# Two output projections: plain float32 products in place of hi and lo parts

## The chip, the cores and the metric

The kernel runs on one core of a Trainium2 chip. The metric is the device time of one execution in microseconds (us); the median of the runs is compared.

## What is computed

Two transformer layers over 512 latent tokens and 256 context tokens, 1024 wide, all in float32. Layer 0 mixes tokens by grouped-query attention (16 heads of 64), layer 1 by latent attention (16 heads, values of 64). What matters here is the product behind each attention and the normalization after it:

```python
y_lat = block_attention(q_lat, k_all, v_all) @ w_o
y_ctx = block_attention(q_ctx, k_ctx, v_ctx) @ w_o if need_ctx else None
...
x = layer_norm(alpha * x + g_a * y_lat, ln_g[i, 0], ln_b[i, 0])
x = layer_norm(alpha * x + g_m * sq_relu_mlp(x * (1.0 + sc_m) + sh_m, mlp_w1[i], mlp_w2[i]), ...)
```

`w_o` is 1024 x 1024 in each layer. Layer 0 needs latent and context rows (768 tokens), layer 1 latent rows alone (512).

## The kernel before

Tokens are handled in tiles of 128: six in layer 0 (`range(NT)`), four in layer 1 (`range(NCT, NT)`). Most products keep float32 accuracy by splitting each operand into a hi part, a cast to float32r by ScalarE (`split_hi`, line 62), and a lo part, the float32 value less that cast, by VectorE (`split_lo`, line 65). Three products replace one: hi by hi, hi by lo, lo by hi (`mm3`, lines 88 to 91). Two kinds of work on TensorE use float32 as it is: the transposes (line 707 and others), and the attention's values (line 731), which multiply 64 columns for each of two heads into the two halves of one PSUM tile.

**Weights.** A weight goes by SP's DMA queue into one of three buffers named `raw` (line 69); its hi and lo parts go into rings of six `wh` and six `wl` tiles (lines 79 and 80). A slot is taken again when its last reader is done.

**The attention** (`Attn.run`, line 752) is a loop of rounds: scores of 128 queries for two heads, softmax, transposes of the probabilities, values. The order on TensorE is the program's; the other engines are ordered by the scheduler. At given steps of the loop (`at`) other work is put in. `early_weights` (lines 656 to 671) uses this: six of the eight 512 KB pieces of `w_o` are loaded (line 660) and some steps later split (lines 665 and 666, kept in program order). Result tiles `o`, one for each of eight head pairs, are 128 partitions by token tile by 128.

**The output projection** (`out_proj`, lines 881 to 936) has the eight pieces of the sum in `wts`; the last two are loaded and split into a pool of their own (line 904). For every token tile, the eight result pieces are split into `oh` and `ol` (lines 896 to 902), then for each k six products of 128 columns by 512 are summed in two PSUM tiles (lines 911 to 919):

```python
for k in range(KD):
    wh, wl = wts[k]
    for hf in range(2):
        ...
        nc.tensor.matmul(acc[hf], oh[k], wh[:, cs], start=(k == 0), stop=False)
        nc.tensor.matmul(acc[hf], oh[k], wl[:, cs], start=False, stop=False)
    for hf in range(2):
        ...
        nc.tensor.matmul(acc[hf], ol[k], wh[:, cs], start=False, stop=(k == KD - 1))
```

Behind them come the gate (line 924), the residual (line 925), the normalization (lines 304 to 314), the store of the row for later (line 929), and, for every two tiles, transposes and modulation into the MLP's operand (`to_act`, lines 331 to 362), which run in the time of the next tile. The MLP's first products (lines 975 to 979) follow on TensorE; its weights take the next slots of the same `wh` and `wl` rings.

Of the kernel before, what the change touches and what calls it, by code (L numbers as in the profile page):

```python
# [11 lines left out]
F32 = mybir.dt.float32  # L12
F32R = mybir.dt.float32r
# [6 lines left out]
P = 128  # L20
# [7 lines left out]
KD = D // P  # L28
# [11 lines left out]
def backbone(ctx, tc, a, out):  # L40
# [3 lines left out]
    nc = tc.nc  # L44

    def pool(stack, name, bufs=1, side="left", space=None):
        kw = {"space": space} if space is not None else {"side": side}
        return stack.enter_context(tc.tile_pool(name=name, bufs=bufs, reuse_waits="tile", **kw))

    const = pool(ctx, "const")  # L50
    wpool = pool(ctx, "wpool")
# [6 lines left out]
    def one():  # L58
        return ps.tile([P, 512], F32, name="one", tag="one", bufs=4)

    def split_hi(dst, src):
        return nc.scalar.copy(out=dst, in_=src)  # L62

    def split_lo(dst, src, hi):
        return nc.vector.tensor_tensor(out=dst, in0=src, in1=hi.bitcast(F32), op=ALU.subtract)  # L65

    def raw_tile(src, n):
        raw = wpool.tile([P, 1024], F32, name="raw", tag="raw", bufs=3)
        nc.sync.dma_start(raw[:, 0:n], src)
        return raw  # L70

    def weight(src, n=1024, wp=None, tiles=None, gate=None):
        raw = raw_tile(src, n)
        if gate is not None:
            nc.gpsimd.tensor_tensor(out=raw, in0=raw, in1=gate, op=ALU.mult)
        if tiles is not None:
            wh, wl = tiles
        elif wp is None:
            wh = wpool.tile([P, 1024], F32R, name="wh", tag="wh", bufs=6)
            wl = wpool.tile([P, 1024], F32R, name="wl", tag="wl", bufs=6)  # L80
        else:
            wh = wp.tile([P, 1024], F32R, name="wxh", tag="wxh", bufs=2)
            wl = wp.tile([P, 1024], F32R, name="wxl", tag="wxl", bufs=2)
        split_hi(wh[:, 0:n], raw[:, 0:n])
        split_lo(wl[:, 0:n], raw[:, 0:n], wh[:, 0:n])
        return wh, wl
# [278 lines left out]
    def stream(t):  # L365
        return 1 if t < NCT else 0
# [260 lines left out]
    for ch in range(1, 3):  # L627
        wts = [weight(a["w_qkv"][ch * 4 + i]) for i in range(4)]
        started.close()
        for t in range(NT):  # L630
            if (ch, t) in in_pairs:
                if t % 2 == 0:
                    pair = big()
                acc = pair[:, t % 2, :]
            else:
                acc = one()
# [10 lines left out]
            if kraw:  # L647
                kt, raw = kraw.popitem()
# [4 lines left out]
                assert not late  # L653
                st_k.close()

    def early_weights(src, ws, n, i0, i1, step, at):


        def load(k):
            ws.append(raw_tile(src[k], 1024))  # L660

        def split(k):
            raw = ws[k]
            wh, wl = (wpool.tile([P, 1024], F32R, name=nm, tag=nm, bufs=6) for nm in ("wh", "wl"))
            tc.keep_in_program_order(split_hi(wh, raw))
            tc.keep_in_program_order(split_lo(wl, raw, wh))
            ws[k] = wh, wl

        for k in range(n):
            at.setdefault(i0 + step * k, []).append(lambda k=k: load(k))  # L670
            at.setdefault(i1 + step * k, []).append(lambda k=k: split(k))

    class Attn:

# [182 lines left out]
    for k in range(KD):  # L857
        t = wpool.tile([P, D], F32, name="ada", tag="wh" if k < 6 else "wl", bufs=6)
# [6 lines left out]
    w_o0, at = [], {}  # L865

    for i, f in enumerate(ada_pe(0, 4, ada_ts, ada_bias4)):
        at.setdefault(0 + i, []).append(f)

    early_weights(a["w_o0"], w_o0, 6, 40, 46, 5, at)  # L870
    att.run(
        (0, QS0), prep0, scores0, lambda kt, h: V[:, kt, (h // 4) * 64 : (h // 4) * 64 + 64], o_of0, 8,
        ctx_scores0, fill, at,
# [7 lines left out]
    def out_proj(layer, wsrc, early, tiles, col0, o_of, x_src, x_dst, wxp, aH, aL, A, B, lnst, zst, x_ln):  # L881

        zp = pool(zst, "zp", side="right")
        ln = LN(lnst, layer, 0, 2, 1)
        if x_ln is not None:
            ln.gain(x_ln)
        wts = early + [weight(wsrc[k]) for k in range(len(early), 6)]
        temp = lambda: zp.tile([P, 512], F32, name="v", tag="v", bufs=2)  # L890
        ln.gate_tile(stream(tiles[0]))
        zs, late = [], []
        for t in tiles:
            s = stream(t)
            oh, ol = [], []
            for k in range(KD):
                h = ln.lp.tile([P, P], F32R, name="oh", tag="oh", bufs=12)
                l = ln.lp.tile([P, P], F32R, name="ol", tag="ol", bufs=12)
                split_hi(h, o_of(k)[:, t, :])
                split_lo(l, o_of(k)[:, t, :], h)  # L900
                oh.append(h)
                ol.append(l)
            if len(wts) < KD:
                wts += [weight(wsrc[k], wp=wxp) for k in range(6, KD)]
            z = zp.tile([P, D], F32, name="z", tag="z", bufs=3)
            x = ln.x_tile(x_src(t))
            if x_ln is not None:
                ln.affine(x, x)
            g = ln.gate_tile(s)
            acc = [one(), one()]  # L910
            for k in range(KD):
                wh, wl = wts[k]
                for hf in range(2):
                    cs = slice(hf * 512, hf * 512 + 512)
                    nc.tensor.matmul(acc[hf], oh[k], wh[:, cs], start=(k == 0), stop=False)  # L915
                    nc.tensor.matmul(acc[hf], oh[k], wl[:, cs], start=False, stop=False)  # L916
                for hf in range(2):
                    cs = slice(hf * 512, hf * 512 + 512)
                    nc.tensor.matmul(acc[hf], ol[k], wh[:, cs], start=False, stop=(k == KD - 1))  # L919
            while late:  # L920
                late.pop(0)()
            for hf in range(2):
                cs = slice(hf * 512, hf * 512 + 512)
                nc.vector.tensor_tensor(out=z[:, cs], in0=acc[hf], in1=g[:, cs], op=ALU.mult)
            nc.vector.scalar_tensor_tensor(
                out=z, in0=x, scalar=ALPHA, in1=z, op0=ALU.mult, op1=ALU.add
            )
            ln.norm(z)
            nc.sync.dma_start(x_dst[t * P : (t + 1) * P, :], z)
            zs.append(z)  # L930
            if len(zs) == 2:
                col = (t - 1) * P - col0
                late += ln.to_act(zs, col, s, A, B, aH, aL, temp, pin=t == tiles[-1])
                zs = []
        ln.close_x()
        return late
# [158 lines left out]
    A01, B01 = mod_ab(0, 1, 0)  # L1095
    st_ln, st_z = ExitStack(), ExitStack()
    late = out_proj(0, a["w_o0"], w_o0, range(NT), 0, o_of0, x_rows, xres[0], wx, aH, aL, A01, B01, st_ln, st_z, None)
    st_ln.close()
    st_wx.close()
# [105 lines left out]
    for t in range(NCT, NT):  # L1205
        acc = one()
        cols = slice(t * P, (t + 1) * P)
        for k in range(KD):
            wh, wl = wcq[k // 2]
# [58 lines left out]
    for t in range(NT):  # L1268
        cols = slice(t * P, (t + 1) * P)
        for hf in range(2):  # L1270
            acc = one()
            cs = slice(hf * 512, hf * 512 + 512)
# [39 lines left out]
    for c in range(4):  # L1312
        for j in range(2):
            q1[2 * c + j] = qo.tile([P, NLT, 192], F32, name=f"q1_{2 * c + j}", tag="qo1", bufs=9)
        for t in range(NLT):
# [5 lines left out]
            acc = one()  # L1321
            cols = slice(t * P, (t + 1) * P)
            for k in range(3):
                u = c * 3 + k
                wh, wl = wuq[u // 2]
# [36 lines left out]
    def o_of1(pr):  # L1362
# [2 lines left out]
        return o1[pr]  # L1365

    w_o1, at = [], {}
    early_weights(a["w_o1"], w_o1, 6, 20, 25, 6, at)
    att.run(first1, prep1, scores1, lambda kt, h: V1[:, kt, h * 64 : h * 64 + 64], o_of1, 8, None, None, at)
    st_att.close()  # L1370
    st_aq.close()
# [6 lines left out]
    A11, B11 = mod_ab(1, 1, 2)  # L1378
    st_ln, st_z = ExitStack(), ExitStack()
    late = out_proj(  # L1380
        1, a["w_o1"], w_o1, range(NCT, NT), CTX, o_of1, lambda t: xres[1][t * P : (t + 1) * P, :], xres[2], wx,
        aH, aL, A11, B11, st_ln, st_z, 1,
# [120 lines left out]
```

## Time and profile before

| | |
|---|---|
| three runs | 1687.68, 1688.68, 1694.34 us (median 1688.68) |
| the profiled execution | 1685.56 us, of which the span is 1683.8 |
| mean granted TensorE clock | 0.991 |

The span runs from the first to the last instruction; the 1.76 us between it and the execution's own time lie around it. Engines are PE (TensorE's products), PEld (its weight loads), DVE (VectorE), ACT (ScalarE), POOL (GpSimd) and SP (the queue that issues the DMAs). Starts of products are measured, their ends are modelled, so the spacing of starts tells more than a duration. A view that gives "idle before" names in brackets how long the engine stood and what ended that.

### The profile page before, as it was taken

How to read it: one execution, taken by the hardware profiler on the slowest of the kernel's cores; microseconds unless marked ns; L12 is line 12 of the kernel's file. 1: busy time of each engine (PE TensorE's matmuls, PEld its weight loads, DVE VectorE, ACT ScalarE, POOL GpSimd, SP SyncE). 2: the span in 40 equal slices, each digit the busy share in tenths (PEclk: the TensorE clock that was granted, in tenths of full speed). 3: DMA queues.
4: the chain of work that ended last, by engine and by line, in shares of the span. 5: the costliest groups of instructions: out<-in, count | busy, mean ns of one | idle time of the engine just before them, and what ended most of it. 6: DMA issues, size and time to landing. Idle time of an engine off the chain costs nothing.

```text
span 1683.8 us, 23748 instructions
## 1 busy us (share of the span) xinstructions
PE 1620.3 (96%) x9266; PEld 1364.3 (81%) x9266; DVE 1113.3 (66%) x1700; ACT 721.6 (43%) x1317; POOL 449.4 (27%) x317
## 2 busy tenths in 40 slices
PE   8997998999999999999999899999999899999996
PEld 6875776788888888998899798888878788888884
DVE  4778788766656775556448766766658655555577
ACT  3324677645532453342121356666653522222221
POOL 0247889000422444233104531000004200000034
PEclk9999999999999999999999999999999999999998
DMA  8312112223443464443122222001022432332322
GB/s 321 140 64 94 58 52 100 83 94 130 159 138 100 138 198 166 138 140 135 64 75 72 73 94 91 1 1 38 26 99 103 162 101 100 100 100 88 100 75 76
DMA packets 51969, 172.05 MB, mean 102 GB/s; under 512 B 6776, under 2 KB 6928, under 8 KB 51856
## 3 DMA queue, kind: packets, MB, share of 16 engines
q1 hardware_dynamic: 51824, 170.51, 30.1%
q8 instruction: 73, 1.20, 0.3%
q14 instruction: 40, 0.33, 0.1%
q10 hardware_dynamic: 32, 0.02, 0.0%
HBM read 161.03 MB, written 9.47 MB: 101 GB/s over the span
## 4 chain that ended last, share of the span: by engine, by line
PE 78%; DVE 11%; ACT 4%; DMA 3%; POOL 2%; issue 1%; DVEq 0%; SPq 0%; ACTq 0%; POOLq 0%
PE one L89 9%; PE one L91 9%; PE one L90 9%; PE big L975 7%; PE big L979 7%; PE big L978 7%; PE one L731 6%; PE one L707 4%; PE one L915 2%; DVE wl L65 2%; PE one L919 2%; PE one L916 2%; POOL xr L208 2%; DMA raw<-in_mlp_w_dram 2%; DVE yacc L1059 1%
## 5 line engine op out<-in xcount | busy, mean ns | idle before, releaser
L62 ACT CAST wh<-raw 128x1024 fp32r<-128x1024 f32 (+3 forms) x172 | 171.9, 1016 | 399.7 <-PE one L91 213.9
L65 DVE TENSOR_TENSOR wl<-raw,wh 128x1024 fp32r<-128x1024 f32 (+3 forms) x172 | 218.2, 1283 | 169.1 <-ACT wh L62 167.8
L975 PE MATMUL big<-actH,wh 128*128 128x384 f32 (+2 forms) x800 | 280.5, 351 | 4.8 <-ACT wh L62 4.8
L979 PE MATMUL big<-actH,wl 128*128 128x384 f32 (+2 forms) x800 | 279.6, 350 | 0.6 <-DVE wl L65 0.6
L978 PE MATMUL big<-actL,wh 128*128 128x384 f32 (+2 forms) x800 | 279.6, 350 | 0.0
L89 PE MATMUL one<-wh,hh 128*128 128x512 f32 x640 | 256.1, 401 | 11.3 <-ACT hh L62 6.8
L90 PE MATMUL one<-wl,hh 128*128 128x512 f32 x640 | 255.7, 400 | 1.3 <-DVE wl L65 1.3
L91 PE MATMUL one<-wh,hl 128*128 128x512 f32 x640 | 254.5, 399 | 2.1 <-DVE hl L65 2.1
L1057 DVE TENSOR_TENSOR yacc<-yacc,one 128x512 f32<-128x512 f32 x260 | 174.4, 683 | 112.2 <-PE one L91 111.9
L208 POOL TENSOR_TENSOR xr<-xr,raw 128x1024 f32<-128x1024 f32 x49 | 129.3, 2639 | 243.4 <-ACT raw L206 227.7
L975 PEld LDWEIGHTS big<-actH,wh 128*128 128x128 f32 x800 | 150.1, 188 | 18.5 <-ACT wh L62 6.0
L979 PEld LDWEIGHTS big<-actH,wl 128*128 128x128 f32 x800 | 150.1, 188 | 13.6 <-DVE wl L65 1.0
L978 PEld LDWEIGHTS big<-actL,wh 128*128 128x128 f32 x800 | 150.2, 188 | 12.2 <-issue 0.4
L89 PEld LDWEIGHTS one<-wh,hh 128*128 128x128 f32 x640 | 122.1, 191 | 42.7 <-ACT hh L62 7.9
L91 PEld LDWEIGHTS one<-wh,hl 128*128 128x128 f32 x640 | 121.3, 190 | 31.6 <-DVE hl L65 2.8
L90 PEld LDWEIGHTS one<-wl,hh 128*128 128x128 f32 x640 | 122.0, 191 | 27.6 <-DVE wl L65 1.7
L328 POOL TENSOR_TENSOR xr<-xr,ln_g 128x1024 f32<-128x1024 f32 x14 | 36.7, 2622 | 391.8 <-PE one L919 242.0
L691 ACT ACTIVATE prob<-big,nm 128x768 f32<-128x768 f32 x128 | 115.9, 909 | 56.2 <-DVE nm L690 55.9
L690 DVE TENSOR_REDUCE nm<-big 128x1 f32<-128x768 f32 x128 | 119.5, 953 | 14.7 <-PE big L1358 8.6
L707 PE MATMUL one<-ident,prob 128*128 128x128 f32 x832 | 103.2, 273 | 1.7 <-ACT pT L710 1.7
L707 PEld LDWEIGHTS one<-ident,prob 128*128 128x128 f32 x832 | 94.9, 141 | 5.2 <-ACT pT L710 2.2
L731 PE MATMUL one<-pT,V 128*64 128x256 f32 x768 | 96.8, 387 | 2.1 <-DVE pT L712 2.1
(245 smaller groups left out, 2823.4 us busy)
## 6 DMA issues: line engine op xcount, KB each, us to landing
raw<-in_mlp_w_dram SPq DMA_DIRECT2D x128, 512.0 KB
raw<-in_w_ada_dram SPq DMA_DIRECT2D x56, 512.0 KB
sraw<-in_w_ada_dram SPq DMA_DIRECT2D x16, 512.0 KB
araw<-in_w_ada_dram SPq DMA_DIRECT2D x32, 256.0 KB
raw<-in_w_o_dram SPq DMA_DIRECT2D x16, 512.0 KB
xr<-xres SPq DMA_DIRECT2D x14, 512.0 KB
raw<-in_w_qkv_dram SPq DMA_DIRECT2D x12, 512.0 KB
xres<-z SPq DMA_DIRECT2D x10, 512.0 KB
```

Of the source, the lines that this page charges most:

```text
L62: return nc.scalar.copy(out=dst, in_=src)
L65: return nc.vector.tensor_tensor(out=dst, in0=src, in1=hi.bitcast(F32), op=ALU.subtract)
L89: nc.tensor.matmul(o, lh, rh, start=start, stop=False)
L90: nc.tensor.matmul(o, lh, rl, start=False, stop=False)
L91: nc.tensor.matmul(o, ll, rh, start=False, stop=stop)
L208: nc.gpsimd.tensor_tensor(out=accs[s], in0=accs[s], in1=dst, op=ALU.add)
L707: nc.tensor.transpose(tp[:, j * P : (j + 1) * P], pts[j % 2][:, k * P : (k + 1) * P], ident)
L731: nc.tensor.matmul(acc[64 * hh : 64 * hh + 64, 0:256], v(kts[n], hh), PT[:, :, n, hh, :], start=(n == 0), stop=(n == len(kts) - 1),)
L975: mm = nc.tensor.matmul(o, wh[:, ks], aH[:, k, s:e], start=(k == 0), stop=False)
L978: nc.tensor.matmul(o, wh[:, ks], aL[:, k, s:e], start=False, stop=False)
L979: nc.tensor.matmul(o, wl[:, ks], aH[:, k, s:e], start=False, stop=(k == KD - 1))
L1057: nc.vector.tensor_tensor(out=yacc[i][:, cs], in0=yacc[i][:, cs], in1=accs[hf], op=ALU.add)
```

## The change

Operands of both output projections stay float32. The pieces of `w_o` are loaded by the new `o_weight` straight into slots of the rings, the first six under the tag `wh`, the last two under `wl`; `raw` is not used for them. The splits of the weights and of the attention's results go, and with them the second set of steps of `early_weights`. In layer 0 one product takes 128 columns; in layer 1 two products of 64 columns write the two halves of the PSUM tile's partitions.

```diff
-    def early_weights(src, ws, n, i0, i1, step, at):
-        def load(k):
-            ws.append(raw_tile(src[k], 1024))
-        def split(k):
-            raw = ws[k]
-            wh, wl = (wpool.tile([P, 1024], F32R, name=nm, tag=nm, bufs=6) for nm in ("wh", "wl"))
-            tc.keep_in_program_order(split_hi(wh, raw))
-            tc.keep_in_program_order(split_lo(wl, raw, wh))
-            ws[k] = wh, wl
+    def o_weight(src, k):
+        w = wpool.tile([P, 1024], F32, name="wo", tag="wh" if k < 6 else "wl", bufs=6)
+        nc.sync.dma_start(w, src)
+        return w
+
+    def early_weights(src, ws, n, i0, step, at):
         for k in range(n):
-            at.setdefault(i0 + step * k, []).append(lambda k=k: load(k))
-            at.setdefault(i1 + step * k, []).append(lambda k=k: split(k))
+            at.setdefault(i0 + step * k, []).append(lambda k=k: ws.append(o_weight(src[k], k)))
...
-    early_weights(a["w_o0"], w_o0, 6, 40, 46, 5, at)
+    early_weights(a["w_o0"], w_o0, 6, 40, 5, at)
...
-        wts = early + [weight(wsrc[k]) for k in range(len(early), 6)]
+        wts = early + [o_weight(wsrc[k], k) for k in range(len(early), KD)]
...
+        m = 64 if layer else P
         for t in tiles:
             s = stream(t)
-            oh, ol = [], []
-            for k in range(KD):
-                h = ln.lp.tile([P, P], F32R, name="oh", tag="oh", bufs=12)
-                l = ln.lp.tile([P, P], F32R, name="ol", tag="ol", bufs=12)
-                split_hi(h, o_of(k)[:, t, :])
-                split_lo(l, o_of(k)[:, t, :], h)
-                oh.append(h)
-                ol.append(l)
-            if len(wts) < KD:
-                wts += [weight(wsrc[k], wp=wxp) for k in range(6, KD)]
...
             for k in range(KD):
-                wh, wl = wts[k]
                 for hf in range(2):
                     cs = slice(hf * 512, hf * 512 + 512)
-                    nc.tensor.matmul(acc[hf], oh[k], wh[:, cs], start=(k == 0), stop=False)
-                    nc.tensor.matmul(acc[hf], oh[k], wl[:, cs], start=False, stop=False)
-                for hf in range(2):
-                    cs = slice(hf * 512, hf * 512 + 512)
-                    nc.tensor.matmul(acc[hf], ol[k], wh[:, cs], start=False, stop=(k == KD - 1))
+                    for i in range(0, P, m):
+                        nc.tensor.matmul(
+                            acc[hf][i : i + m], o_of(k)[:, t, i : i + m], wts[k][:, cs],
+                            start=(k == 0), stop=(k == KD - 1),
+                        )
...
-    early_weights(a["w_o1"], w_o1, 6, 20, 25, 6, at)
+    early_weights(a["w_o1"], w_o1, 6, 20, 6, at)
```

## Rows read from the trace of the kernel before

**Rows 1.** The page, parts 1 (busy, share, instructions) and 4 (chain by engine).

```profile
PE 1620.3 (96%) x9266; PEld 1364.3 (81%) x9266; DVE 1113.3 (66%) x1700; ACT 721.6 (43%) x1317; POOL 449.4 (27%) x317
...
PE 78%; DVE 11%; ACT 4%; DMA 3%; POOL 2%; issue 1%; DVEq 0%; SPq 0%; ACTq 0%; POOLq 0%
```

**Rows 2.** Windows of both output projections; columns as its first line says.

```profile
core 0: us, PE busy (x) PEld busy (x) DVE busy (x) ACT busy (x) POOL busy (x), PEclk, DMA share, GB/s
1252.70:1298.70 46.00, 46.00 (x206) 37.13 (x205) 37.04 (x65) 20.19 (x46) 21.01 (x11) 1.00 0.38 133
329.00:399.00 70.00, 70.00 (x316) 56.56 (x315) 41.25 (x103) 30.17 (x71) 2.77 (x5) 1.00 0.32 112
```

**Rows 3.** TensorE's timeline (start, us, what): first products of both projections, and behind.

```profile
328.46 0.51 PE L915 MATMUL one<-wh,oh 128*128 128x512 f32 x1 [0.72 <-ACT oh L62]
...
399.91 0.34 PE L975 MATMUL big<-actH,wh 128*128 128x384 f32 x1
...
1251.98 0.51 PE L915 MATMUL one<-wh,oh 128*128 128x512 f32 x1 [0.71 <-ACT oh L62]
...
1298.93 0.28 PE L975 MATMUL big<-actH,wh 128*128 128x256 f32 x1
```

**Rows 4.** The chain in order of time (start, us): transposes inside the projections.

```profile
386.86 1.81 PE one L341 x16
...
1285.94 1.81 PE one L341 x16
```

**Rows 5.** TensorE's timeline, one group of values, cut at three places.

```profile
318.23 0.44 PE L731 MATMUL one<-pT,V 128*64 128x256 f32 x2
...
318.23 0.87 PE L731 MATMUL one<-pT,V 128*64 128x256 f32 x6
...
318.23 1.51 PE L731 MATMUL one<-pT,V 128*64 128x256 f32 x12
```

**Rows 6.** Line 707, transposes: all records (ns min/median/max), and one group.

```profile
L707 PEld LDWEIGHTS one<-ident,prob x832: 137/141/146, 133.5 to 1246.0; 128*128 128x128 f32 x167
L707 PE MATMUL one<-ident,prob x832: 270/272/331, 133.6 to 1246.1; 128*128 128x128 f32 x167
...
312.74 1.47 PE L707 MATMUL one<-ident,prob 128*128 128x128 f32 x12
```

**Rows 7.** The chain in order of time, layer 0's attention: weight subtractions.

```profile
256.81 1.13 DVE wl L65
...
279.81 2.08 DVE wl L65
```

**Rows 8.** TensorE's timeline at those two places: where it stood idle.

```profile
257.70 0.55 PE L610 MATMUL one<-ident,q 128*128 128x128 f32 x3 [0.75 <-ACT pT L710]
...
282.54 1.52 PE L731 MATMUL one<-pT,V 128*64 128x256 f32 x12 [1.30 <-DVE pT L712]
286.07 0.33 PE L152 MATMUL one<-ident,modrow 128*128 128x128 f32 x1 [1.41 <-DVE modrow L132]
```

**Rows 9.** Window of layer 1's attention around one early split; columns as in rows 2.

```profile
1140.00:1165.00 25.00, 24.64 (x173) 20.44 (x172) 16.84 (x24) 16.66 (x36) 0.00 (x0) 1.00 0.07 22
```

**Rows 10.** TensorE's timeline: the last product with a key weight.

```profile
1210.56 0.34 PE L91 MATMUL one<-CKH,wl 128*128 128x384 f32 x1
```

**Rows 11.** VectorE's timeline before layer 0's MLP; the chain inside layer 1's MLP.

```profile
397.43 1.23 DVE L65 TENSOR_TENSOR wl<-raw,wh 128x1024 fp32r<-128x1024 f32 x1 [0.86 <-ACT wh L62]
...
1318.85 4.55 DVE wl L65 x2
```

**Rows 12.** Timeline of products and weight loads at 328.80.

```profile
328.80 0.39 PE L916 MATMUL one<-wl,oh 128*128 128x512 f32 x1
328.80 0.19 PEld L915 LDWEIGHTS one<-wh,oh 128*128 128x128 f32 x1
```

**Rows 13.** Windows with the granted clock; columns as in rows 2.

```profile
130.00:135.00 5.00, 2.52 (x24) 1.60 (x16) 4.94 (x13) 3.46 (x10) 2.76 (x3) 1.00 0.75 306
135.00:140.00 5.00, 3.44 (x27) 1.95 (x27) 4.91 (x12) 2.31 (x9) 2.53 (x3) 0.75 0.00 0
...
1241.90:1251.90 10.00, 9.37 (x77) 6.11 (x75) 3.16 (x7) 5.24 (x13) 0.00 (x0) 1.00 0.00 0
```

## The prediction

> **What bounds the kernel now.** The page first: TensorE is busy 96% of the span and holds 78% of the chain that ended last, while VectorE holds 11% [rows 1]. So what counts is TensorE's own time, and elsewhere only what TensorE waits for. Then the stretches of the two output projections by engine: TensorE is busy 70.00 of 70 us and 46.00 of 46 us, at the full granted clock, with VectorE at 59% and 81% and ScalarE below half [rows 2]. Inside them nothing that ScalarE, VectorE or a transfer does is waited for, so an instruction taken from those engines there buys nothing by itself. Last, the TensorE timeline gives the price of the work: layer 0 runs from 328.46 to 399.91, layer 1 from 1251.98 to 1298.93 [rows 3], with two and one groups of 16 transposes of 1.81 us in between [rows 4] (layer 0's other group is equal). That leaves 71.45 - 3.62 = 67.83 us for 6 tiles x 8 k x 6 = 288 products, 0.2355 us each, and 46.95 - 1.81 = 45.14 us for 4 x 8 x 6 = 192, 0.2351 us each.
>
> **The change, part by part.**
>
> 1. *Layer 0's products.* 288 products of hi and lo parts become 6 x 8 x 2 = 96 plain float32 products of 128x128 by 512. The trace has no such product, so its price comes from the plain float32 products of the attention values (line 731): 64 columns by 256, two side by side, six of them per group. There each product leaves two records (12 in a group). The busy time of a group seen up to its 2nd record is 0.44 us, up to its 6th 0.87 us [rows 5]: every two records more, one on each half of the array, cost 0.215 us. Both halves work at once, so one record over 256 columns takes 0.215 us, and over 512 columns 0.43 us. The nearest row for 128 columns are the float32 transposes: 12 records in 1.47 us, the last of which shows 0.27 us, so 1.20 / 11 = 0.109 us per 128 columns [rows 6], the same rate. I take 0.43 us per record and two records per product: 96 x 2 x 0.43 = 82.6 us, against 67.8 us: **+14.7 us**. Bounds for the record: below, 0.2355 us, what a product of hi and lo parts takes over the same 512 columns; above, 0.43 + 0.14 = 0.57 us, if the weight load (0.14 us in the transposes [rows 6]) did not hide. I am near neither end, because the values and the transposes agree on the rate and both load weights under the running product.
>
> 2. *Layer 1's products.* 4 x 8 x 2 = 64 units of two 64-column products, two records each: 64 x 2 passes, both halves at once. This is the form of the values with twice the columns: 128 x 0.43 = 55.0 us against 45.1: **+9.9 us**. Bounds: 0.43 for a pair of records, and 0.86 if the halves ran one after the other, which rows 5 exclude.
>
> 3. *The splits of the attention outputs* (lines 898 to 902, 8 casts and 8 subtractions a tile) and those of weights 6 and 7. They go from ScalarE and VectorE, off the path by rows 2. What they do cost is the entry: TensorE stands 0.72 and 0.71 us before its first product, waiting for the first cast [rows 3]. The new first product reads head pair 0 as the attention wrote it, long before; pair 7, the late one, is needed only at k = 7. **-1.4 us**, between -1.4 and 0 (if the order puts another wait there).
>
> 4. *The six early weight splits inside each attention.* In layer 0 two of the subtractions are on the chain, 1.13 and 2.08 us [rows 7], and TensorE stands 0.75, 1.30 and 1.41 us at those places [rows 8]. With them gone the next late ones there are the row maximum and the copies of the transposed probabilities on VectorE. **-3.2 us**, the two pieces; bounds 0 (the next late ones end no sooner) and -3.5 (the idle time of rows 8). In layer 1 TensorE is busy 24.64 of 25 us in a stretch with such a split [rows 9]: 0.
>
> 5. *The loads.* The same 16 loads stay on SP's queue, now straight into the slots of hi and lo weights. They no longer wait for a split to free one of three raw buffers, so nothing behind them comes later for that. One new wait: in layer 1 the fifth and sixth load take the slots of the two key weights, which the last key product reads at 1210.56 [rows 10]. SP stands until then, and what is queued behind is the next output weights and the first MLP weights, all wanted from 1251.98 on [rows 3]; 41 us cover them. 0.
>
> 6. *The start of each MLP.* Its first hi slot comes free when the last tile has used weight 0, as before. In layer 0 the second of its lo parts was finished at 398.66, 1.25 us before TensorE came to it [rows 11]; the last tile now takes 2.4 us longer (14.7 / 6), so this cover grows. In layer 1 a VectorE wait of 4.55 us on lo parts lies inside the MLP [rows 11], after the part that changes: it stays, though its company on GpSimd can shift, which I take as 0 with +-4 us.
>
> Sum: 14.7 + 9.9 - 1.4 - 3.2 = **+20.0 us**. The profiled execution took 1685.56 us (span 1683.8), 3.1 us under the median of the runs, 1688.68. I start between the two, at 1687, and forecast **1707 us**.
>
> One rule of the Trainium skill would make this dearer. In the timeline the load for the next product starts at 328.80, together with the running product of 0.39 us, on the same 128 rows [rows 12], so loads are hidden here. "TensorE: Matmul & The Clock Gate" (Part 3, The mechanism) has the load overlap running products only when they use other row groups. The trace does not bear that out for this kernel's products; no row shows it for a 128-column float32 product of 512. By the rule the sum would be that of the second rival below instead of 1707 us.
>
> **The rivals.**
>
> - *Side of faster: a 128-column float32 product costs one record.* The transposes are 128-column float32 work and leave one record each [rows 6], where the values leave two. If layer 0's products did too, it would take 96 x 0.43 = 41.3 us, 26.5 us less than now, and the kernel 1687 - 26.5 + 9.9 - 4.6 = 1666 us. Against it: a transpose only passes data through, and every true float32 product in the trace leaves two. It decides once a product is cheaper than (67.8 + 4.6 - 9.9) / 96 = 0.65 us, and is faster by over 0.5% below 0.56 us. Chance 0.05.
> - *The weight load does not hide* under a 128-column float32 product: 192 x 0.14 = 27 us more in layer 0, 1734 us. For: such products were never run here. Against: rows 6 and 12. Chance 0.05.
> - *The clock falls.* TensorE's granted clock fell to 1.2 GHz, the lower of its two levels, behind a stretch in which it was busy 2.52 of 5 us: the mean of the next 5 us is 0.75 of full [rows 13]. If plain float32 products of layer 0 did not hold the upper level, they would take twice as long: 1707 + 82.6 = 1790 us. Against: from 1241.9 to 1251.9 TensorE did float32 products and transposes only, and the clock stayed at 1.00 [rows 13]; that is 10 us, with 64-column products, not 80 us with 128. Chance 0.06.
> - *More comes back than I count:* the splits slow the attention beyond the two pieces on the chain, and give back 12 us or more of the 24.6: some 1690 us, no change to be measured. Against it stand rows 9 and how little idle time there is. Chance 0.05.
>
> **How the numbers follow.** The forecast has 0.79 and its own range is 1699 to 1719: steps 3 and 4 can give back 4.6 us less or 0.3 more, step 6 is open by 4 either way, and the three runs shown lie from 1.0 below to 5.7 above their median. With the near edge of the fourth rival, and with a load that shows in part, it becomes 1695 to 1724; outside are the first three rivals. A measurement tells about 0.5%, 8.4 us, from no change: 1680 to 1697. Faster 0.05 (first rival), same 0.05 (fourth), slower 0.90.
>
> **What would show it.** Right: two records per product at layer 0's line, 0.43 us apart at clock 1.00, TensorE busy through both stretches, layer 0's stretch about 86 us and layer 1's about 57 with their transposes, no idle time before the first product, and no weight subtraction in the attention chain. Wrong: one record per product; records 0.57 us apart; a clock under 1.00 inside layer 0's stretch; TensorE idle at either MLP's start.

## The result and the profile after

The changed kernel took **1706.45 us** (median of 3 runs, 1703.54 to 1708.41) against 1688.68 before: a ratio of 1.0101, with an interval of 1.0084 to 1.0117. The two medians lie 17.8 us apart, and the forecast of 1707 us was missed by 0.6 us. The profiled execution took 1703.54 us (span 1701.7) and was the fastest of the three.

The page after, parts 1 and 4, answers to [rows 1]:

```profile
PE 1642.6 (97%) x9234; PEld 1327.4 (78%) x9234; DVE 1071.9 (63%) x1604; ACT 686.8 (40%) x1221; POOL 444.8 (26%) x317
...
PE 76%; DVE 12%; ACT 4%; DMA 3%; POOL 2%; issue 2%; DVEq 0%; SPq 0%; ACTq 0%; POOLq 0%
```

TensorE is busy 22.3 us longer with 32 records fewer; VectorE loses 41 us and ScalarE 35 us of work. So the trade was made as the diff says: work came off two engines with room and went onto the one without.

Next the windows of after, one from each stage's first TensorE instruction to that of the next: layer 0's attention, its output projection, its MLP, and the same three of layer 1 (columns as the first line says).

```profile
core 0: us, PE busy (x) PEld busy (x) DVE busy (x) ACT busy (x) POOL busy (x), PEclk, DMA share, GB/s
128.51:323.03 194.52, 181.90 (x1424) 141.76 (x1422) 154.07 (x261) 124.50 (x308) 141.63 (x125) 0.99 0.22 75
323.03:411.40 88.37, 88.37 (x247) 41.24 (x243) 32.99 (x61) 18.75 (x28) 2.76 (x5) 1.00 0.24 85
411.40:966.33 554.93, 543.32 (x2744) 483.62 (x2743) 350.95 (x376) 196.05 (x213) 173.39 (x72) 0.99 0.38 125
1071.05:1261.15 190.10, 187.47 (x1315) 155.61 (x1315) 118.57 (x174) 122.81 (x269) 0.00 (x0) 1.00 0.04 15
1261.15:1320.51 59.36, 59.36 (x284) 21.72 (x282) 24.53 (x35) 12.16 (x18) 20.40 (x11) 1.00 0.26 93
1320.51:1701.67 381.16, 361.49 (x1650) 294.84 (x1648) 234.05 (x288) 110.42 (x147) 47.84 (x23) 0.99 0.31 102
```

Beside the same stretches of before:

| stretch, us | before | after | difference |
|---|---|---|---|
| layer 0: attention | 200.75 | 194.52 | -6.2 |
| layer 0: projection | 71.45 | 88.37 | +16.9 |
| layer 0: MLP | 555.21 | 554.93 | -0.3 |
| layer 1: attention | 192.09 | 190.10 | -2.0 |
| layer 1: projection | 46.95 | 59.36 | +12.4 |
| layer 1: MLP to the end | 384.84 | 381.16 | -3.7 |

Both projections stay at 100% TensorE and clock 1.00, as in [rows 2], while VectorE falls to 37% and 41% in them. The TensorE timeline of after (start, us, what, and in brackets the idle time before) shows where the borders moved:

```profile
253.89 0.55 PE L610 MATMUL one<-ident,q 128*128 128x128 f32 x3 [0.50 <-DVE pT L706]
276.21 0.55 PE L610 MATMUL one<-ident,q 128*128 128x128 f32 x3 [0.51 <-DVE pT L706]
284.02 0.33 PE L152 MATMUL one<-ident,modrow 128*128 128x128 f32 x1 [0.82 <-DVE modrow L132]
...
323.03 8.85 PE L900 MATMUL one<-wo,o 128*128 128x512 f32 x20
331.72 0.27 PE L152 MATMUL one<-ident,modrow 128*128 128x128 f32 x1
331.92 1.52 PE L725 MATMUL one<-pT,V 128*64 128x256 f32 x12
333.37 0.44 PE L734 MATMUL one<-ident,rb 128*128 128x128 f32 x2
...
397.31 14.00 PE L900 MATMUL one<-wo,o 128*128 128x512 f32 x32
...
411.40 0.42 PE L959 MATMUL big<-actH,wh 128*128 128x384 f32 x1
...
1261.15 0.59 PE L900 MATMUL one<-wo,o 128*64 128x512 f32 x1
1261.16 0.65 PE L725 MATMUL one<-pT,V 128*64 128x256 f32 x2
...
1306.58 14.00 PE L900 MATMUL one<-wo,o 128*64 128x512 f32 x64
1320.51 0.39 PE L959 MATMUL big<-actH,wh 128*128 128x256 f32 x1
```

The first products need no cast any more, so they start without idle time, where [rows 3] had 0.72 and 0.71 us. They even start ahead of the attention's last values (line 725): some 1.9 us of values and transposes in layer 0 and 1.2 us in layer 1 now lie inside the projection's stretch. So an attention and its projection must be read together: **+10.7 us in layer 0** (16.9 - 6.2) and **+10.4 us in layer 1** (12.4 - 2.0). The first three lines answer to [rows 8]: of the idle times 0.75, 1.30 and 1.41 us there stand 0.50, 0.51 and 0.82.

The chain of after in order of time (start, us, what) holds every product of both projections:

```profile
323.11 8.78 PE one L900 x20
...
333.81 32.62 PE one L900 x76
366.43 1.75 PE one L341 x16
368.17 27.53 PE one L900 x64
395.71 1.75 PE one L341 x16
397.46 13.86 PE one L900 x32
...
1261.32 0.27 PE one L900
...
1261.80 0.37 PE one L900
...
1262.82 2.79 PE one L900 x12
...
1265.98 38.77 PE one L900 x178
1304.75 1.90 PE one L341 x16
1306.65 13.93 PE one L900 x64
```

Layer 0: 20 + 76 + 64 + 32 = 192 records, two for each of 96 products, in 82.79 us. In the long piece one takes 32.62 / 76 = 0.429 us. Layer 1: 178 records in its long piece, 89 pairs, in 38.77 us, 0.436 us a pair on average; step 2 below shows where that is more than 0.429.

### The profile page after: what moved, and what is told of

Read it like the earlier page. It is cut to its first block, busy times and chain, and to the rows that moved or that the text cites. A ratio compares the mean times of both kernels' runs of the same rounds, so it can differ in the third digit from the quotient of the medians.

```text
span 1701.7 us, 23378 instructions
## 1 busy us (share of the span) xinstructions
PE 1642.6 (97%) x9234; PEld 1327.4 (78%) x9234; DVE 1071.9 (63%) x1604; ACT 686.8 (40%) x1221; POOL 444.8 (26%) x317
## 4 chain that ended last, share of the span: by engine, by line
PE 76%; DVE 12%; ACT 4%; DMA 3%; POOL 2%; issue 2%; DVEq 0%; SPq 0%; ACTq 0%; POOLq 0%
PE one L89 9%; PE one L91 9%; PE one L90 9%; PE one L900 8%; PE big L959 7%; PE big L963 7%; PE big L962 6%; PE one L725 6%; PE one L701 3%; POOL xr L208 2%; DVE wl L65 2%; DMA raw<-in_mlp_w_dram 2%; DVE nm L684 2%; DVE yacc L1043 1%; PE big L846 1%
## 5 line engine op out<-in xcount | busy, mean ns | idle before, releaser
L62 ACT CAST wh<-raw 128x1024 fp32r<-128x1024 f32 (+3 forms) x160 | 159.1, 1013 | 399.2 <-PE one L91 215.0
L65 DVE TENSOR_TENSOR wl<-raw,wh 128x1024 fp32r<-128x1024 f32 (+3 forms) x160 | 201.4, 1275 | 168.6 <-ACT wh L62 167.5
L900 PE MATMUL one<-wo,o 128*64 128x512 f32 (+1 forms) x448 | 140.3, 593 | 0.0
L900 PEld LDWEIGHTS one<-wo,o 128*64 128x64 f32 (+1 forms) x448 | 55.6, 160 | 79.1 <-issue 77.9
```

The lines of the kernel that those rows point to most:

```text
L900: nc.tensor.matmul(acc[hf][i : i + m], o_of(k)[:, t, i : i + m], wts[k][:, cs], start=(k == 0), stop=(k == KD - 1),)
```

## The experiments

Two theories stood. Mine: the products are the cost, layer by layer, and the early splits give a little back in layer 0's attention alone. Against it: the cost or the gift lies elsewhere, in the width of the products, in the stalls, or in the MLP behind.

**One layer at a time.** The first kernel has layer 0 as changed and layer 1 as before; the second the other way round. In both the old and new forms of the product loop stand side by side:

```diff
-            for k in range(KD):
+            for k in range(KD if plain else 0):
...
+                            acc[hf][i : i + m], o_of(k)[:, t, i : i + m], wts[k][:, cs],
...
+            for k in range(0 if plain else KD):
                 wh, wl = wts[k]
```

> Layer 0 as changed, layer 1 as before. Theory (TensorE pays 0.43 us per record, two records per product, and the attention of layer 0 gives back its stalls): the layer 0 part alone. In the changed kernel's trace layer 0's attention and projection together took 10.7 us longer (194.52 + 88.37 against 200.75 + 71.46), so about +10.7 us, some 1699 us. Rival (most of the slowdown comes from layer 1 or from the MLP starts): under +5 us.

> Layer 1 as changed, layer 0 as before. Theory: layer 1's attention and projection took 10.4 us longer together (190.10 + 59.36 against 192.09 + 46.95), so +10.4 us less up to 3.7 that the MLP behind may give back as in the changed kernel's trace: +7 to +10 us, 1695 to 1699. If the two parts are independent, the gains of this run and of the layer 0 run add up to the change's +17.8. Rival (the two parts share something, a ring or the clock): the sum is off by more than 5 us.

Measured: 1696.68 us, 1.0057 (1.0035 to 1.0078) for layer 0 alone, and 1699.04 us, 1.0047 (1.0020 to 1.0073) for layer 1 alone. Together 1.04%, against 1.01% for the whole change: the two parts add up, as far as intervals of some 0.2% either way can tell. By stretch the first has 193.41 + 88.37 in layer 0 and 192.07 + 46.95 in layer 1; the second has 200.58 + 71.48 and 190.07 + 59.36. Each layer's attention and projection show their own part, +9.6 and +10.4 us, and no other.

**The width of the products.** One line sets it:

```diff
-        m = 64 if layer else P
+        m = P
```

and, in the other kernel, `m = 64`.

> The changed kernel with 128 columns in layer 1 too. Theory (a record costs 0.43 us whatever its width, and halves side by side take as long as one whole): 64 products of two records, 55 us, the same as now: within 3 us of the changed kernel. Rival (two 64-column products side by side are what keeps layer 1 cheap: with 128 columns the weight load shows or the clock falls): 128 x 0.14 = 18 us more, or 55 us more at the lower clock.

> The changed kernel with two 64-column products side by side in layer 0 too. Theory: 192 passes of 0.43 us as now, within 3 us of the changed kernel. Rival (64-column pairs are cheaper than one 128-column product): layer 0's stretch shorter than 84 us by more than 3 us; or dearer by the change between column groups, by as much.

Measured: all 128 wide 1705.71 us, 1.0100 (1.0080 to 1.0121); all in pairs of 64, 1712.15 us, 1.0131 (1.0109 to 1.0154). Layer 1's projection takes 58.53 us with 128 columns against 59.36 with pairs; layer 0's 89.82 us with pairs against 88.37. The groups by line and form of the all-64 kernel, around layer 0's projection (count, busy us, mean ns of one):

```profile
L900 PE MATMUL one<-wo,o 128*64 128x512 f32 x384 | 84.2, 593 | 0.0
```

The same row of after:

```profile
L900 PE MATMUL one<-wo,o 128*128 128x512 f32 x192 | 83.3, 594 | 0.0
```

Twice the records, each as long as a wide one, in nearly the same busy time: both halves of the array work at once, and the split into halves saves nothing and costs 1.5 us at most. The expectation for the all-64 kernel missed even so: its median lies 5.7 us above that of the changed kernel, where 3 was the limit. Its projection of layer 0 grew by only 1.5 us, less than the rival of dearer pairs asked, so the other 4 us are not in its products. Its record shows more stretches at a lower granted clock than that of after (160 to 170 us at 0.83 in layer 0's attention against 1.00, and 1360 to 1370 us at 0.66 in layer 1's MLP), which come and go from run to run, as the section on steps shows; whether the pairs make them likelier was not settled.

**The early splits, put back as idle work.** The changed kernel, with a cast and a subtraction of each early weight at their old places in both attentions; nothing reads their results:

```diff
+    def dead(w):
+        dh, dl = (wpool.tile([P, 1024], F32R, name=nm, tag="wl", bufs=6) for nm in ("dh", "dl"))
+        tc.keep_in_program_order(split_hi(dh, w))
+        tc.keep_in_program_order(split_lo(dl, w, dh))
...
+            at.setdefault(i1 + step * k, []).append(lambda k=k: dead(ws[k]))
```

> The changed kernel with the twelve early weight splits put back into both attentions as work whose results nobody reads. Theory (the splits are what stalled TensorE in layer 0's attention, 4.6 us of idle time in the kernel before; in layer 1 they cost nothing): +4 to +5 us over the changed kernel, all of it in layer 0's attention, with VectorE's subtraction back in the chain there. Rival (the stalls went because the raw buffers and SP's queue are freer): the attention of layer 0 stays as short as in the changed kernel, within 1 us.

Measured: 1710.11 us, 1.0120 (1.0089 to 1.0151), 3.7 us over the change's median. In its profiled execution layer 0's attention takes 201.07 us (194.52 in after), layer 1's 190.02 us (190.10). The idle times came back where they were, in its TensorE timeline:

```profile
260.57 0.55 PE L610 MATMUL one<-ident,q 128*128 128x128 f32 x3 [0.74 <-ACT pT L710]
262.09 2.35 PE L731 MATMUL one<-pT,V 128*64 128x256 f32 x12 [0.97 <-DVE pT L712]
...
285.80 0.55 PE L610 MATMUL one<-ident,q 128*128 128x128 f32 x3 [0.75 <-ACT pT L710]
287.46 1.52 PE L731 MATMUL one<-pT,V 128*64 128x256 f32 x12 [1.11 <-DVE pT L712]
...
290.99 0.33 PE L152 MATMUL one<-ident,modrow 128*128 128x128 f32 x1 [1.41 <-DVE modrow L132]
```

0.74 + 0.97 + 0.75 + 1.11 + 1.41 = 4.98 us, against 0.50 + 0.51 + 0.82 = 1.83 in after: 3.15 us are the splits' own. The rest of the 6.5 us goes with two falls of the clock. A group of 12 values takes 2.35 us at 262.09 and 1.52 at 287.46, and the windows (columns as above) show the fall around the first, and an earlier one:

```profile
160.00:170.00 10.00, 7.49 (x51) 5.52 (x50) 7.27 (x13) 4.57 (x11) 8.87 (x9) 0.83 0.16 52
260.00:265.00 5.00, 3.45 (x17) 1.95 (x18) 4.33 (x7) 3.17 (x11) 3.53 (x4) 0.76 0.36 105
```

From 260 to 265 the mean granted clock is 0.76, part of it at the lower level of 1.2 GHz, behind the two idle times; it is 1.00 at the same place in after. In before, the same idle times passed without it, so this part is no fixed price of the splits. The fall between 160 and 170 (1.00 in after) can't be theirs: the first cast put back starts at 248.7 us, and the all-64 kernel, which has none, fell at the same place. The medians alone would not settle this: the intervals of this run and of the change overlap, and the profiled execution, 1716.94 us, is the slowest of four. That the splits stall layer 0's attention, and layer 1's not at all, is shown by the idle times; that they can bring the clock down is seen once.

**The splits moved, the products kept.** If the early splits cost 3 us, can they be had back without the dearer products? Before, with layer 0's weights left raw during the attention, its first tile multiplied as plain float32, and the splits under those products:

```diff
-    early_weights(a["w_o0"], w_o0, 6, 40, 46, 5, at)
+    early_raw(a["w_o0"], w_o0, 6, 40, 5, at)
...
+                    nc.tensor.matmul(
+                        acc[hf], o_of(k)[:, t, :], raws[k][:, cs], start=(k == 0), stop=(k == KD - 1)
+                    )
...
+                split_hi(wh, raws[k])
+                split_lo(wl, raws[k], wh)
```

> The kernel before, but layer 0's weights come in raw during the attention, the first token tile is multiplied as plain float32, and the splits are done under its products; the other five tiles and layer 1 use hi and lo parts as before. Theory: the attention gives back its 4.6 us and the entry 0.7, tile 0 costs 16 x 2 x 0.43 - 48 x 0.2355 = 2.5 us more: -2.8 us against the kernel before, 0.2%, so at the edge of what can be told. Rival (the splits, crowded into 14 us, make tile 1 wait): 0 to +5 us.

Measured: 1687.65 us over 12 runs against 1688.46, 0.9995 (0.9981 to 1.0008). Layer 0's attention gains 6.6 us (194.17) and its projection loses 4.4 (75.89): 2.2 us in the stretches, and nothing that the whole time can tell from no change. As in after, 1.9 us of the last values lie inside the projection here, so the attention gave back 4.7 and the projection cost 2.5. TensorE is busy 75.89 of 75.89 us in it: no tile waited for the splits.

**The products taken away.** Before with all splits, but the hi x hi products alone: the products with either lo part are left out.

```diff
-                    nc.tensor.matmul(acc[hf], oh[k], wh[:, cs], start=(k == 0), stop=False)
-                    nc.tensor.matmul(acc[hf], oh[k], wl[:, cs], start=False, stop=False)
...
-                    nc.tensor.matmul(acc[hf], ol[k], wh[:, cs], start=False, stop=(k == KD - 1))
+                    nc.tensor.matmul(acc[hf], oh[k], wh[:, cs], start=(k == 0), stop=(k == KD - 1))
```

> The kernel before with all splits, but only the products of hi parts by hi parts; it leaves out the two products with lo parts in both projections. Theory (both stretches are TensorE's alone, and its time follows the number of records): two thirds of 67.8 + 45.1 us go, -75 us, if nothing else becomes the bound; the normalization of a tile on VectorE and ScalarE, some 6 us a tile, would then be longer than the 3.8 us of products and leave about -50 us. Rival (the stretches are held by VectorE or transfers, and TensorE only looks busy): under -20 us.

Measured: 1666.65 us, 0.9866 (0.9842 to 0.9891): 22 us less, though two thirds of the products, 320 of 480, are 75 us by the prices above. This expectation missed. Layer 0's projection falls from 71.45 to 51.66 us, layer 1's from 46.95 to 42.26. Of its profile, a window of layer 0's projection (columns as above):

```profile
328.00:376.00 48.00, 28.51 (x114) 22.57 (x114) 35.80 (x99) 24.86 (x68) 2.73 (x5) 0.79 0.46 162
```

and its chain in order of time:

```profile
329.41 7.32 DMA gate<-gates
...
343.27 3.46 DMA gate<-gates
```

TensorE is busy 28.51 of 48 us, and the mean granted clock of the window is 0.79. What binds now is first the load of the gates, which the projection used to cover, then mostly VectorE's work on each tile. So "TensorE alone bounds the projection" holds for dearer products, and for cheaper ones only some 20 us down in layer 0 and 5 in layer 1.

**One cast, one product.** What remains if the lo parts go altogether: operands cast once to float32r, no subtraction, one product. All lo parts are left out, so the operands are rounded.

```diff
-            wh, wl = (wpool.tile([P, 1024], F32R, name=nm, tag=nm, bufs=6) for nm in ("wh", "wl"))
+            wh = wpool.tile([P, 1024], F32R, name="wh", tag="wh", bufs=6)
...
-            tc.keep_in_program_order(split_lo(wl, raw, wh))
```

> Operands of both projections cast once to float32r, one product each; it leaves out the lo parts of weights and results, their splits and their products. Against the run that kept all splits and only dropped the products (1666.65 us), VectorE loses some 80 subtractions of about 0.2 us in the projections and 16 of 1.2 us. Theory (with a third of the products the projections are held by VectorE's normalization and by the first gate's transfer, and the early subtractions stall layer 0's attention): layer 0's attention gives back 4 to 6 us, the projections some 4 to 8 together: 1653 to 1659 us. Rival (the gate's transfer and the casts hold them alone): only the attention's 4 to 6 us come, 1661 to 1663.

Measured: 1648.31 us against 1690.03, 0.9763 (0.9732 to 0.9794), 5 us below the range that was expected. Layer 0's projection takes 43.35 us, layer 1's 37.70: against the run before, 12.9 us come from the two projections, where 4 to 8 were expected. VectorE is less busy in the projection without the subtractions: the window of layer 0's shows it at 26.63 of 44 us, TensorE at 31.89, the clock at 0.83. What gave the surplus was not taken apart.

```profile
322.00:366.00 44.00, 31.89 (x156) 24.08 (x153) 26.63 (x54) 26.49 (x71) 3.69 (x5) 0.83 0.47 168
```

The chain there is led by the load of the gates with 22.1%, ahead of TensorE's products with 10.2%. It is faster than both kernels, at the price of the lo parts' precision; within the precision of hi and lo parts, or of float32, no kernel here beat the one before.

## Why the prediction was right

**Step 1, layer 0's products: +14.7 predicted.** The chain gives 82.79 us for the 192 records, against 82.6. The price was read off the values of [rows 5], half as many columns on half the width, and it carried over.

**Step 2, layer 1's products: +9.9.** The chain's pieces of line 900 add up to 0.27 + 0.37 + 2.79 + 38.77 + 13.93 = 56.1 us, against 55.0. The price of a pair held. The TensorE timeline of after, the long piece cut at three places and its end:

```profile
1269.82 0.60 PE L900 MATMUL one<-wo,o 128*64 128x512 f32 x2
...
1269.82 15.62 PE L900 MATMUL one<-wo,o 128*64 128x512 f32 x72
...
1269.82 30.64 PE L900 MATMUL one<-wo,o 128*64 128x512 f32 x142
...
1303.73 1.02 PE L900 MATMUL one<-wo,o 128*64 128x512 f32 x2
```

From the 72nd to the 142nd record 35 pairs take 30.64 - 15.62 = 15.02 us, 0.429 us a pair, like one record of 128 columns. One pair is busy 0.60 us where one record takes 0.59; in the trace its second record starts 6 to 7 ns behind the first. The Trainium skill has this offset, in "TensorE: Matmul & The Clock Gate" (Part 3, The mechanism): tiles of one array start about 4 ns apart and the span grows by that for each further tile. The trace agrees in kind for one pair, with 6 to 7 ns, but in a row of pairs the offset is not paid again. The missing microsecond lies where records are not side by side. The last two of the long piece take 1.02 us, 0.59 + 0.43, one behind the other; and the first 14, among the attention's last values, take 0.27 + 0.37 + 2.79 = 3.43 us, where seven pairs take 3.0. The all-128 kernel, which has no pairs, needs 0.83 us less for the whole stretch (59.36 - 58.53).

**Step 3, the entry: -1.4.** Both idle times are gone. That the products would move ahead of the last values was not foreseen; TensorE does the same work in another order, and what shows of a cost are the 0.4 us of layer 1's first 14 records.

**Step 4, the early splits: -3.2 in layer 0, 0 in layer 1.** In before the idle times at these splits add up to 4.55 us (the 0.75, 1.30 and 1.41 of [rows 8], and 0.35 and 0.74 right beside them); in after 1.83 are left: -2.7. So the size was 0.5 us too large; the step had taken VectorE's two pieces on the chain for the gain. The second part of the step held: of the two next late ones that it named, it was the copy of the transposed probabilities, 0.50 us each time (line 706). With the splits back, 3.15 us of idle time came back in layer 0 and nothing in layer 1.

Steps 1, 3 and 4 together say +10.8 us for layer 0's attention and projection, where the stretches show +10.7; for layer 1, +9.2, where they show +10.4. In layer 0 the agreement to 0.1 is partly luck. By the rows the products cost 82.79 - 67.83 = +15.0, and the splits gave back 2.7. One more idle time of before, which no step counted, went too:

```profile
325.60 0.33 PE L152 MATMUL one<-ident,modrow 128*128 128x128 f32 x1 [0.45 <-DVE modrow L132]
```

In after the same instruction, at 331.72, stands behind 20 products and waits for nothing. 15.0 - 0.7 - 2.7 - 0.45 = +11.1; the other 0.4 us were not traced.

Luck is also in the 0.6 us of the total. The steps add up to +20.0, and the medians differ by 17.8; the forecast started from 1687, which is 1.7 us under the median of before, and the two nearly cancel. The range of 1699 to 1719 is a little off from the terms that it names, which give 1702 to 1721; the result lies in both.

**Step 5, the loads: 0.** TensorE is busy 88.37 of 88.37 and 59.36 of 59.36 us, so no weight was waited for.

**Step 6, the MLP starts: 0, +-4 in layer 1.** Neither MLP starts with idle time. Layer 1's came out 3.7 us shorter, but not through the change. Windows of before, the whole stretch and two parts of it:

```profile
1298.93:1683.77 384.84, 364.23 (x1649) 297.04 (x1647) 235.23 (x290) 110.46 (x147) 48.08 (x23) 0.98 0.31 103
1335.00:1340.00 5.00, 5.00 (x16) 3.81 (x15) 2.12 (x2) 3.29 (x7) 0.00 (x0) 0.66 0.40 116
1652.50:1657.50 5.00, 4.72 (x14) 3.72 (x15) 1.47 (x3) 0.83 (x2) 0.00 (x0) 0.66 0.47 152
```

Twice part of this stretch ran at the lower clock level in before (a mean of 0.66 over 5 us, which is at most 0.34 x 5 = 1.7 us of full speed lost each time); after has no such place, its clock is 1.00 from 1320.51 to 1690. That accounts for at most 3.4 of the 3.7 us. The same wait stands before the second fall in before and at the same product in after, where no fall followed:

```profile
1652.78 0.58 PE L89 MATMUL one<-wh,hh 128*128 128x512 f32 x1 [3.28 <-ACT hh L62]
...
1672.65 0.50 PE L89 MATMUL one<-wh,hh 128*128 128x512 f32 x1 [3.31 <-ACT hh L62]
```

The kernels with the same code in this stretch and layer 1's projection changed speak for chance too: 384.38 us in the all-128 kernel, 384.64 with the idle splits and 385.34 in the all-64 kernel, each with such falls (0.66 from 1345 to 1355 in the first), and 381.76 with layer 1 alone changed, at 1.00 up to the same last part. It fits that the profiled execution of after, 2.9 us under its median, has a mean clock of 0.995 and the other two runs 0.991 and 0.992.

**The rivals.** *One record per product*: 192 records stand in the row of line 900. *Loads that don't hide*: the timeline of weight loads in after, inside layer 0's last tile,

```profile
397.85 0.19 PEld L900 LDWEIGHTS one<-wo,o 128*128 128x128 f32 x1 [0.24 <-issue]
398.28 0.19 PEld L900 LDWEIGHTS one<-wo,o 128*128 128x128 f32 x1 [0.24 <-issue]
```

has a load of 0.19 us every 0.43 us, each under a running product of the same 128 rows, with 0.24 us to spare. The rule of the Trainium skill that was weighed there ("TensorE: Matmul & The Clock Gate", Part 3, The mechanism), by which a load overlaps a running product only on other row groups, does not hold for these products: the sum by it was 1734 us, the run gave 1706. (The same section excepts a load into the background weight buffer; whether that is what happens here no run can show.) *The clock*: 1.00 in both projections of after, over 88 and 59 us of plain float32; nothing speaks for a fall under such products. It fell instead where the projection got cheaper and TensorE stood idle, to 0.79 in the hi x hi kernel. *More given back by the splits*: 2.7 us and not 12. (As the prediction puts it, 12 of the 24.6 us back would have made 1700 us; its 1690 takes some 22.)

## What to carry to other kernels

Where a stretch shows TensorE at 100%, price a change there by TensorE's records alone and treat what it takes off other engines as worth only the idle time it ends. A float32 product took two records of 0.429 us over 512 columns, 0.86 us, three hi and lo products of float32r 0.71 us: the three are cheaper, as long as their casts are hidden. A bound found this way holds in the dearer direction; in the cheaper one, look up what the bound has been covering (here the load of the gates, within 20 us) before counting on the gain.

## What was not expected of the hardware

Two 64-column float32 records side by side took as long as one 128-column record, 0.429 us, and the projections in pairs came out 0.8 and 1.5 us longer: here nothing was to be had by splitting the array for products with full 128 columns. Records of 64 columns also run beside each other when they belong to different work: at 1261.16 a record of values (line 725) starts within 10 ns of a product of the projection (line 900).

Falls of the granted clock, each worth up to some 1.7 us, were there in one kernel and not in another over the same code, and two of them are as much as step 4 was worth. So a difference of 3 us between two profiled executions can be read only after the clock of both has been compared.
